# A two-layer diffusion backbone on one core: the recurrence's triangles loaded ahead of all rows, its rows a step ahead of its scores, the modulation read out by ScalarE, and the second layer's gated projections first

## The chip, the cores and the metric

The kernel runs on one core of a Trainium2 chip. The metric is the device time of one execution in microseconds (us); the program before has a median of 2315.48 us over three runs, from 2312.57 to 2316.03 us. The engines have short names: PE is TensorE (matmuls), PEld its weight loads, DVE is VectorE, ACT is ScalarE, POOL is GpSimd and SP is SyncE, which here only issues transfers. Each engine works through its own list of instructions in a fixed order.

## The reference

Two layers work on 512 latent tokens and 256 context tokens of width 1024. Each layer modulates its normalised input by a vector computed from the conditioning, projects it once, and feeds three token mixers: a bidirectional recurrence (RWKV-7), latent attention and windowed attention. Each mixer's result is gated, projected, merged and added back. All in fp32. Cut to what the change touches:

```python
mod = jax.nn.silu(c) @ ada_w + ada_b          # 3072 values for the latent tokens, and again for the context
shift, scale, gate = jnp.split(mod[:, None, :], 3, axis=-1)
h = rms_norm(x, norm_g) * (1.0 + scale) + shift
za, ga, zb, gb, zc, gc, zg = jnp.split(h @ w_in, list(IN_CUTS), axis=-1)
ya, yac = rwkv7_branch(za, zac, ...)          # the recurrence
def step(S, inp):                             # per token, per head, both directions
    r_t, w_t, k_t, v_t, kk_t, a_t = inp
    sa = jnp.einsum('bhvk,bhk->bhv', S, kk_t)
    S = (S * w_t[:, :, None, :] - sa[..., None] * (kk_t * a_t)[:, :, None, :]
         + v_t[..., None] * k_t[:, :, None, :])
    return S, jnp.einsum('bhvk,bhk->bhv', S, r_t)
```

## The kernel before

**Projections.** Every weight tile is loaded (L165), rounded by ScalarE to a high part `wh` (L168) and subtracted by GpSimd to a low part `wl` (L169); a product of fp32 numbers is then three matmuls into the PSUM tile `g` (`hh` by `wh`, `hl` by `wh`, `hh` by `wl`). `proj` copies `g` out to a tile `st`: a plain copy by ScalarE (L789) for the inputs of the attentions, tanh by ScalarE (L791) and a multiply-add by VectorE (L793) for the gates `ga`, `gb`, `gc`. It then stores `st` (L795). One call of `pace(n)` emits n steps of these projections; a step of the second layer is three matmuls of 512 columns. They are the filler with which the recurrence is interleaved.

**The recurrence** (`rwkv`) works in 12 chunks of 64 tokens, four to a group. For a chunk `rwkv_scores` loads the rows `BK` and `AR` (L625 to L634) and `UV` (L635, L636), multiplies them on PE into `scps`, masks those on VectorE (L656, L658), then transposes `BK` on PE into `bkp` (L664). For a group `rwkv_inverse` loads its triangles `TT` in four transfers (L674, L675), transposes them on VectorE (L681), inverts them in 60 dependent VectorE instructions (L690, L692), transposes back (L695, L696), copies a part on ScalarE (L698), and finishes on PE (`zp`, `yp`). `rwkv_step` carries the state from chunk to chunk: `Rp`, `Up`, `Sp`, `Yp` on PE with copies between. `readout` normalises finished rows and stores them.

**The modulation** (`ada`) runs beside this. The first layer's first four parts are computed at the start with a pool of their own; the other 16 rounds (four of the first layer, twelve of the second) are spread among the filler of the first layer. A round is PE products into `modps`, a copy of them to `row` (L269), four short matmuls with the constant `sum4`, and an add of the bias into `mod` (L277 or L280); both the copy and the add are VectorE's. The two halves of one PSUM bank take turns.

**Order.** A scheduler orders each engine by priority bands; inside `in_line()` PE takes the matmuls in the order in which the code emits them. `FILL[l]` says how many filler steps come ahead of the recurrence and inside each of its parts:

```python
FILL = ((48, 48, 2, (2, 2, 2), (3, 3, 3), 2), (72, 56, 4, (2, 2, 2), (3, 3, 3), 2))
```

Its fourth entry holds for the first three chunks of a group, three parts in each; the fifth for the last chunk. SP issues nearly all loads and stores from one list, so a transfer that waits for a buffer holds up those behind it.

Of the kernel before, what the change touches and what calls it, by code (L numbers as in the profile page):

```python
# [32 lines left out]
FILL = ((48, 48, 2, (2, 2, 2), (3, 3, 3), 2), (72, 56, 4, (2, 2, 2), (3, 3, 3), 2))  # L33
# [27 lines left out]
def build(tc, A, out):  # L61
# [165 lines left out]
    def ada(l, pp, mod, parts, pool=None):  # L227
# [30 lines left out]
        for i_, (q, h) in enumerate((q, h) for q in parts for h in range(512 // n)):  # L258
            ps = bank(i_)

            for k0 in range(0, KT, 4):
                with band(SERVE):
                    ws = four(q, h, k0)
                    for i in range(4):
                        mm(ps[32 * i:32 * i + 32], sc2[:, k0 + i, :], ws[i], start=(k0 == 0), stop=(k0 + 4 == KT),
                           skip_group_check=True)
                yield
            row = spool.tile([P, T], F32, tag="st", name="row", bufs=2)
            V.tensor_copy(row[:, 0:n], ps)  # L269
            nf = n // P  # L270
            pt = ps[:, 0:2 * nf].rearrange("p (f c) -> p f c", c=2)
            for i in range(nf):
                mm(pt[:, i, :], row[:, i * P:(i + 1) * P], C["sum4"])
            if q < 4:
                m, b = (a.rearrange("p (s f) c -> p s f c", s=2)[:, h:h + nf // 2, 2 * q:2 * q + 2]
                        for a in (mod[:, 0:16], pp[:, o:o + 16].unsqueeze(2)))
                V.tensor_tensor(m, pt.rearrange("p (s f) c -> p s f c", s=nf // 2), b.to_broadcast([P, nf // 2, 2, 2]), ALU.add)  # L277
            else:
                f = 4 * q + 2 * h
                V.tensor_tensor(mod[:, f:f + nf], pt, pp[:, o + f:o + f + nf].unsqueeze(2).to_broadcast([P, nf, 2]), ALU.add)  # L280
# [240 lines left out]
    def rwkv(l, D, last, DL, B, pace, zlast):  # L521

        with tc.tile_pool(name="rw", bufs=1, reuse_waits="tile") as rp:
            yo = rp.tile([P, 4, T], F32, name="yo")
            st = {"seen": set(), "S": None}
            parts, YB = {}, {}

            def scores(i):
                if i < NCH:
                    parts[i] = yield from rwkv_scores(l, last, rp, i)  # L530
# [11 lines left out]
            with band(B + 1):  # L542
                rest(scores(0), scores(1))
                ahead = invert(0)
                for _ in range(4):
                    next(ahead)
            with band(B + 4), tc.issue_after(zlast):
                pace(FILL[l][1])
            with band(B + 1), in_line():
# [3 lines left out]
                for i in range(NCH):  # L553
                    if i % NS == 0:
# [4 lines left out]
                        with band(B + 2):  # L559
                            for _ in range(3):  # L560
                                next(ahead, None)
                    nxt = scores(i + 2)
                    step = rwkv_step(l, last, i, yo, st, DL, rp, parts.pop(i), YB[i // NS])
                    for n in FILL[l][3 if i % NS < NS - 1 else 4]:
# [13 lines left out]
    def readout(l, D, rp, yo, part):  # L578
# [10 lines left out]
        tmp = rp.tile([P, 6, 256], F32, tag="AR", name="ro", bufs=4)  # L589
        def spread(p):  # L590
            ps = psum_bcast(256)
            mm(ps, bones, tmp[:, 4 + p % 2])
            V.tensor_scalar(tmp[:, p], ps, 1.0 / 64, None, ALU.mult)

        for p in range(4):
# [4 lines left out]
            S.activation(like(tmp[:, 4 + p % 2], y), y, AF.Square)  # L600
# [18 lines left out]
    def rwkv_scores(l, last, rp, i):  # L619
# [4 lines left out]
        UV = rp.tile([P, 2, 8, 64], F32, tag="UV", name="UV", bufs=4)  # L624
# [7 lines left out]
        else:  # L632
            for par, rows in enumerate(halves):
                DMA.dma_start(AR[rows, :, 2 * par], ar_d[l][rows, i, :, 0])  # L634
        DMA.dma_start(UV[OD, 0], v_d[l][:, i, 0])  # L635
# [844 lines left out]
    for l in range(2):  # L1480
# [18 lines left out]
        def tiles():  # L1499
# [5 lines left out]
            todo = (zb[2:] + zc[4:] + zc[:4] + zb[:2] if last else zb + zc) + ga + gb  # L1505
# [26 lines left out]
        if last:  # L1532
            cctx.close()
            with band(B + 3):
                gqa_tokens(l, F, last, ss)
        rwkv(l, D, last, DL, B, pace, zlast)
        weights["queue"] = getattr(nc, QUEUES[l][2])
        with band(B + 4), tc.issue_after(line["last"]):
            pace(22 * 8 - sum(FILL[l][0:2]) - 2 * FILL[l][2] - NG * (3 * sum(FILL[l][3]) + sum(FILL[l][4])) - 4 * FILL[l][5])
# [163 lines left out]
```

## Time and profile before

| | |
|---|---|
| median of 3 runs | 2315.48 us (2312.57 to 2316.03) |
| the profiled execution's own time | 2317.05 us |
| its span, first to last instruction | 2315.3 us |
| mean granted TensorE clock | 0.953 of full speed |
| PE busy | 2093.6 us, 90% of the span |
| PEld, DVE, ACT, POOL busy | 71%, 54%, 40%, 34% |
| matmuls in the profile | 16648 |
| first load of triangles, first layer | issued 341.66 us into the span |
| first load of triangles, second layer | issued 1583.35 us into the span |

The busy shares are means over stages of very different kinds. The granted clock is the share of full speed that the chip allowed TensorE. Idle time of an engine counts only where that engine holds up the end; in what follows that engine is PE, whose list is nearly full.

### The profile page before, as it was taken

How to read it: one execution, taken by the hardware profiler on the slowest of the kernel's cores; microseconds unless marked ns; L12 is line 12 of the kernel's file. 1: busy time of each engine (PE TensorE's matmuls, PEld its weight loads, DVE VectorE, ACT ScalarE, POOL GpSimd, SP SyncE). 2: the span in 40 equal slices, each digit the busy share in tenths (PEclk: the TensorE clock that was granted, in tenths of full speed). 3: DMA queues.
4: the chain of work that ended last, by engine and by line, in shares of the span. 5: the costliest groups of instructions: out<-in, count | busy, mean ns of one | idle time of the engine just before them, and what ended most of it. 6: DMA issues, size and time to landing. Idle time of an engine off the chain costs nothing. (4 is left out here: it accounts for less than half of the span.)

```text
span 2315.3 us, 42230 instructions
## 1 busy us (share of the span) xinstructions
PE 2093.6 (90%) x16648; PEld 1641.4 (71%) x16648; DVE 1258.3 (54%) x2342; ACT 919.2 (40%) x1694; POOL 787.4 (34%) x646
## 2 busy tenths in 40 slices
PE   6988899888998899999999998799878998998989
PEld 2866667676887777777777876677667876666767
DVE  4457415558435777314776255643667457674742
ACT  3355321233345443443433245542323455444422
POOL 0223112111122444444543323334211145455663
PEclk9999899899999999999999999999989999999999
DMA  7146666555333111455134414567554262115264
GB/s 249 60 134 178 200 197 188 133 147 135 90 105 103 69 46 51 147 165 166 57 102 135 144 51 125 157 209 189 147 117 113 87 214 90 64 50 178 82 196 141
DMA packets 321222, 301.61 MB, mean 130 GB/s; under 512 B 111744, under 2 KB 234368, under 8 KB 321024
## 3 DMA queue, kind: packets, MB, share of 16 engines
q1 hardware_dynamic: 303216, 269.29, 39.0%
q10 hardware_dynamic: 17808, 29.63, 4.0%
q8 instruction: 131, 2.15, 0.4%
q14 instruction: 67, 0.55, 0.1%
HBM read 207.34 MB, written 91.49 MB: 129 GB/s over the span
## 5 line engine op out<-in xcount | busy, mean ns | idle before, releaser
L169 POOL TENSOR_TENSOR wl<-wf,wh 128x512 fp32r<-128x512 f32 x316 | 439.4, 1392 | 1145.3 <-ACT wh L168 1059.4
L157 PE MATMUL g<-hh,wh 128*128 128x512 f32 (+1 forms) x1264 | 468.2, 370 | 11.3 <-DVE st L793 6.3
L157 PE MATMUL g<-hh,wl 128*128 128x512 f32 (+1 forms) x1264 | 454.9, 360 | 9.0 <-POOL wl L169 9.0
L157 PE MATMUL g<-hl,wh 128*128 128x512 f32 (+1 forms) x1264 | 453.0, 358 | 0.0
L168 ACT CAST wh<-wf 128x512 fp32r<-128x512 f32 x316 | 195.0, 619 | 419.5 <-PE g L157 183.6
L157 PEld LDWEIGHTS g<-hh,wh 128*128 128x128 f32 x1264 | 249.2, 197 | 59.1 <-issue 10.2
L157 PEld LDWEIGHTS g<-hh,wl 128*128 128x128 f32 x1264 | 248.6, 197 | 46.1 <-POOL wl L169 10.2
L157 PEld LDWEIGHTS g<-hl,wh 128*128 128x128 f32 x1264 | 249.3, 197 | 34.9 <-issue 4.7
L924 ACT ACTIVATE pe<-stp 128x256 f32<-128x256 f32 (+2 forms) x224 | 114.2, 521 | 171.2 <-PE stp L157 162.5
L928 POOL TENSOR_TENSOR acc<-acc,pe 128x512 f32<-128x512 f32 (+2 forms) x128 | 143.6, 1122 | 105.8 <-ACT pe L924 89.4
L895 DVE TENSOR_REDUCE mx<-mps 128x1 f32<-128x384 f32 (+2 forms) x256 | 123.7, 532 | 26.5 <-PE mps L157 25.7
L157 PE MATMUL yps<-pe,vh 128*64 128x256 f32 (+1 forms) x704 | 96.1, 379 | 0.0
L157 PE MATMUL g<-yh,wh 128*128 128x512 f32 (+1 forms) x224 | 82.8, 373 | 14.1 <-ACT yh L1387 8.6
L949 DVE RECIPROCAL rec<-sps 128x256 f32<-128x256 f32 (+1 forms) x48 | 71.4, 1489 | 43.6 <-PE sps L157 43.0
L656 DVE TENSOR_TENSOR AR<-scps,cst 64x256 f32<-64x256 f32 x96 | 40.1, 418 | 90.1 <-PE scps L157 89.0
L157 PE MATMUL gc<-hh,wh 128*128 128x512 f32 x192 | 79.2, 412 | 8.9 <-ACT hh L333 4.6
L157 PE MATMUL g<-yl,wh 128*128 128x512 f32 (+1 forms) x224 | 82.9, 372 | 3.0 <-POOL yl L1388 3.0
L157 PE MATMUL g<-yh,wl 128*128 128x512 f32 (+1 forms) x224 | 80.8, 365 | 0.0
L157 PE MATMUL scps<-AR,BK 64*128 64x128 f32 (+1 forms) x768 | 64.0, 293 | 16.7 <-DMA AR<-ard 14.2
L157 PE MATMUL gc<-hl,wh 128*128 128x512 f32 x192 | 78.4, 408 | 0.0
L791 ACT ACTIVATE st<-g 128x256 f32<-128x256 f32 (+1 forms) x108 | 56.5, 523 | 52.6 <-PE g L157 52.1
L157 PE MATMUL gc<-hh,wl 128*128 128x512 f32 x192 | 76.6, 399 | 0.0
(392 smaller groups left out, 4299.8 us busy)
## 6 DMA issues: line engine op xcount, KB each, us to landing
wf<-w_in SPq DMA_DIRECT2D x163, 256.0 KB, 2.9
wf<-ada_w SPq DMA_DIRECT2D x84, 256.0 KB, 4.1
wf<-w_in ACTq DMA_DIRECT2D x77, 256.0 KB, 3.0
bkd<-bk SPq DMA_DIRECT2D x16, 768.0 KB, 5.6
zt<-thzg SPq DMA_DIRECT2D x48, 256.0 KB, 3.3
wf<-w_bo SPq DMA_DIRECT2D x40, 256.0 KB, 3.1
thzg<-st SPq DMA_DIRECT2D x24, 384.0 KB, 2.4
vd<-t SPq DMA_DIRECT2D x64, 96.0 KB, 2.4
```

Of the source, the lines that this page charges most:

```text
L157: queued(TE.matmul(o, l, r, start=start, stop=stop, **kw))
L168: S.copy(wh, w32)
L169: eng.tensor_tensor(wl, w32, wh.bitcast(F32), ALU.subtract)
L656: V.tensor_tensor(AR[oth, pds, 2 * par, :], ps[oth, :, a0:a0 + 64], msk("ms", oth), ALU.mult)
L791: S.activation(t[:, sl], p, AF.Tanh, scale=0.5)
L895: V.tensor_reduce(mx, ps, AX.X, ALU.max)
L924: S.activation(e, st, AF.Exp, scale=scale)
L928: G.tensor_tensor(acc, keep.pop(0, acc), e, ALU.add)
L949: V.reciprocal(rec, sps)
```

## The change

It has five parts. (1) In the 16 later rounds of `ada` the copy to `row` and the add of the bias move from VectorE to ScalarE: one copy, and two activations of two columns each in place of one add of four. (2) The loads of the rows become a function of their own, `rwkv_rows`. The triangles of group 0 are loaded ahead of all rows, and each later chunk's rows are issued one step ahead of its scores. (3) The scratch tile of `readout` shrinks from 6 to 4 blocks and takes its buffer from the tag `BK` (3 buffers) where it took one from `AR` (4 buffers). (4) In the second layer the gate tiles `ga` come after the first four tiles of the filler and ahead of the other ungated ones, and `gqa_tokens`, which prepares the windowed attention, is emitted behind the first `pace` of the recurrence and no longer ahead of it. (5) In the second layer group 0 gets three filler steps in each part and no longer two: nine more steps, taken from those behind the recurrence.

```diff
-FILL = ((48, 48, 2, (2, 2, 2), (3, 3, 3), 2), (72, 56, 4, (2, 2, 2), (3, 3, 3), 2))
+FILL = ((48, 48, 2, ((2, 2, 2),) * 3, (3, 3, 3), 2), (72, 56, 4, ((3, 3, 3), (2, 2, 2), (2, 2, 2)), (3, 3, 3), 2))
...
-            V.tensor_copy(row[:, 0:n], ps)
+            (V.tensor_copy if pool else S.copy)(row[:, 0:n], ps)
...
-            if q < 4:
+            if pool:
...
-                f = 4 * q + 2 * h
-                V.tensor_tensor(mod[:, f:f + nf], pt, pp[:, o + f:o + f + nf].unsqueeze(2).to_broadcast([P, nf, 2]), ALU.add)
+                f = 8 * h + 2 * q if q < 4 else 4 * q + 2 * h
+                for i in range(nf):
+                    S.activation(mod[:, f + i, :], pt[:, i, :], AF.Identity, bias=pp[:, o + f + i:o + f + i + 1])
...
+            def rows(i):
+                if i < NCH:
+                    rows_[i] = rwkv_rows(l, last, rp, i)
...
             with band(B + 1):
+
+                ahead = invert(0)
+                next(ahead)
+                for i in range(2):
+                    rows(i)
                 rest(scores(0), scores(1))
-                ahead = invert(0)
-                for _ in range(4):
+                for _ in range(3):
                     next(ahead)
+                rows(2)
             with band(B + 4), tc.issue_after(zlast):
                 pace(FILL[l][1])
+            beside()
...
+                    rows(i + 3)
                     nxt = scores(i + 2)
...
-                    for n in FILL[l][3 if i % NS < NS - 1 else 4]:
+                    for n in FILL[l][3][i // NS] if i % NS < NS - 1 else FILL[l][4]:
...
-        tmp = rp.tile([P, 6, 256], F32, tag="AR", name="ro", bufs=4)
+        tmp = rp.tile([P, 4, 256], F32, tag="BK", name="ro", bufs=3)
...
-    def rwkv_scores(l, last, rp, i):
+    def rwkv_rows(l, last, rp, i):
...
+        return AR, BK
+
+    def rwkv_scores(l, last, rp, i, AR, BK):
...
-            todo = (zb[2:] + zc[4:] + zc[:4] + zb[:2] if last else zb + zc) + ga + gb
+            todo = zb[2:] + zc[4:] + ga + zc[:4] + zb[:2] + gb if last else zb + zc + ga + gb
...
-            with band(B + 3):
-                gqa_tokens(l, F, last, ss)
-        rwkv(l, D, last, DL, B, pace, zlast)
+
+        def tokens():
+            if last:
+                behind = line["last"]
+                with band(B + 3):
+                    gqa_tokens(l, F, last, ss)
+                line["last"] = behind
+
+        rwkv(l, D, last, DL, B, pace, zlast, tokens)
```

The scheduler turns this into a new order on several engines. Three places follow; line numbers of the changed kernel are some 1 to 19 higher than before (L693 and L694 are the loads L674 and L675, L700 is L681, L709 and L711 are L690 and L692, L714 and L715 are L695 and L696, L717 is L698, L675 and L677 are the masks L656 and L658, L812 and L814 are L793 and L795).

**First place: the first layer, ahead of the recurrence.** SP's list before, around the third and fourth load of the first group's triangles (`TT`); `wf` are weight tiles:

```order
L165 DMA wf<-w_in 128x512 [waits DMAHW6_49,DMAHW1_49,PE_49]
L254 DMA wf<-ada_w 128x2x256 [waits DMAHW2_49,Pool_49]
L674 DMA TT<-ttd_130 32x8x256
L254 DMA wf<-ada_w 128x2x256 [waits DMAHW4_49,PE_49]
L165 DMA wf<-w_in 128x512 [waits DMAHW5_49,PE_49]
L254 DMA wf<-ada_w 128x2x256 [waits DMAHW6_49,DMAHW3_49,Pool_49]
L675 DMA TT<-ttd_130 32x32x32
L795 DMA zbd_121<-st 128x768 [waits Activation_49]
```

and now, where the last load (L694) has moved 37 entries up its list, to just ahead of the store that was issued at 328.70 us before:

```order
L693 DMA TT<-ttd_130 32x8x256
L814 DMA zbd_121<-st 128x768 [waits Activation_49]
L254 DMA wf<-ada_w 128x2x256 [waits DMAHW5_49,Pool_49]
L165 DMA wf<-w_in 128x512 [waits DMAHW3_49,DMAHW2_49,PE_49]
L254 DMA wf<-ada_w 128x2x256 [waits DMAHW4_49,PE_49]
L254 DMA wf<-ada_w 128x2x256 [waits DMAHW6_49,PE_49]
L165 DMA wf<-w_in 128x512 [waits DMAHW1_49,PE_49]
L694 DMA TT<-ttd_130 32x32x32
L814 DMA zbd_121<-st 128x768 [waits DMAHW7_49,Activation_49]
```

VectorE's list now, at the end of that first inverse; before, the masks L656 and L658 of the first two chunks all stood ahead of the inverse:

```order
L709 TENSOR_TENSOR inv<-inv,YB 128x30 [waits DVE_49]
L711 TENSOR_TENSOR YB<-YB,inv 128x30 [waits DVE_49]
L714 STREAM_TRANSPOSE YB<-YB 128x32x32 [waits DVE_49]
L715 STREAM_TRANSPOSE inv<-YB 128x1024 [waits DVE_49]
L675 TENSOR_TENSOR AR<-scps,cst 64x4x64 [waits PE_49]
L677 TENSOR_TENSOR TR<-scps,cst 128x4x64
L675 TENSOR_TENSOR AR<-scps,cst 64x4x64 [waits PE_49]
L677 TENSOR_TENSOR TR<-scps,cst 128x4x64
```

All but the first two masks of these chunks have moved behind the inverse.

**Second place: the first layer, second inverse, at about 468 to 477 us of the profile before.** VectorE's list before, with the add L280 of a modulation round behind the inverse's first transpose back:

```order
L695 STREAM_TRANSPOSE YB<-YB 128x32x32 [waits DVE_49]
L656 TENSOR_TENSOR AR<-scps,cst 64x4x64 [waits DMAHW1_49,PE_49]
L658 TENSOR_TENSOR TR<-scps,cst 128x4x64
L656 TENSOR_TENSOR AR<-scps,cst 64x4x64 [waits PE_49]
L658 TENSOR_TENSOR TR<-scps,cst 128x4x64
L280 TENSOR_TENSOR mod_162<-modps,pp 128x4 [waits PE_49]
L696 STREAM_TRANSPOSE inv<-YB 128x1024 [waits DVE_49]
```

and ScalarE's list now at the same place, with the same round's two activations L281:

```order
L684 COPY BKs<-bkp 128x512 [waits PE_49] x2
L754 COPY Rs<-Rp 128x512 [waits PE_49,Activation_49]
L717 COPY YB<-YB 32x32x32 [waits DVE_49,Pool_49]
L281 ACTIVATE mod_162<-modps,pp 128x2 [waits PE_49]
L281 ACTIVATE mod_162<-modps,pp 128x2
L717 COPY YB<-YB 32x32x32
L760 COPY UV<-Up 64x512 [waits PE_49,Activation_49]
```

The add has moved to ScalarE, where it stands behind the copy L717, which waits for the same transpose.

**Third place: the second layer, ahead of its first inverse.** VectorE's list before:

```order
L431 TENSOR_TENSOR ks<-pr,vT 128x512 [waits PE_49]
L656 TENSOR_TENSOR AR<-scps,cst 64x4x64 [waits PE_49] x8
L793 SCALAR_TENSOR_TENSOR st<-st,g 128x512 [waits DMAHW4_49,DMAHW6_49,DMAHW1_49,Activation_49]
L681 STREAM_TRANSPOSE inv<-TT 128x1024 [waits DMAHW5_49,DMAHW7_49,DMAHW4_49,DMAHW2_49]
L686 MEMSET YB 128x32 [waits Pool_49]
```

and now:

```order
L432 TENSOR_TENSOR ks<-pr,vT 128x512 [waits PE_49]
L812 SCALAR_TENSOR_TENSOR st<-st,g 128x512 [waits DMAHW6_49,DMAHW4_49,Activation_49]
L812 SCALAR_TENSOR_TENSOR st<-st,g 128x512 [waits DMAHW6_49,Activation_49]
L812 SCALAR_TENSOR_TENSOR st<-st,g 128x512 [waits DMAHW5_49,Activation_49]
L812 SCALAR_TENSOR_TENSOR st<-st,g 128x512 [waits DMAHW4_49,Activation_49]
L700 STREAM_TRANSPOSE inv<-TT 128x1024 [waits DMAHW5_49,DMAHW7_49,DMAHW2_49,DMAHW1_49]
L705 MEMSET YB 128x32 [waits Pool_49]
```

The four gate tiles stand ahead of the inverse, and no longer one ahead of it and the others within; the eight masks stand within it now.

## Rows read from the trace of the kernel before

**Rows 1.** The page: PE's and the other engines' busy time, share, instructions.

```profile
PE 2093.6 (90%) x16648; PEld 1641.4 (71%) x16648; DVE 1258.3 (54%) x2342; ACT 919.2 (40%) x1694; POOL 787.4 (34%) x646
```

**Rows 2.** Windows: length, busy of PE, PEld, DVE, ACT, POOL; granted clock; DMA.

```profile
266.00:480.00 214.00, 183.76 (x1761) 140.27 (x1760) 88.30 (x216) 44.67 (x81) 38.41 (x32) 0.92 0.62 174
412.50:422.30 9.80, 9.55 (x155) 7.99 (x156) 1.60 (x5) 2.73 (x5) 0.59 (x1) 0.52 0.32 95
1275.00:1300.00 25.00, 25.00 (x146) 21.77 (x145) 6.63 (x10) 6.30 (x9) 7.80 (x7) 1.00 0.47 158
```

**Rows 3.** PE's waits, 262 to 582 us: total, times, longest.

```profile
PE scps L157 <- DMA AR<-ard: 14.2, 3, 7.3
PE modps L157 <- DMA wf<-ada_w: 7.5, 4, 5.8
PE modps L157 <- DVE mod L280: 6.6, 3, 6.1
...
PE zp L157 <- DVE inv L696: 2.4, 1, 2.4
...
PE g L157 <- DVE st L793: 1.7, 1, 1.7
```

**Rows 4.** PE's waits, 1600 to 1720 us.

```profile
PE zp L157 <- DVE inv L696: 10.8, 1, 10.8
PE zp L157 <- issue: 6.1, 1, 6.1
PE g L157 <- DVE st L793: 4.3, 2, 3.1
```

**Rows 5.** Timeline of VectorE at 263 us: start, duration, instruction, idle before.

```profile
263.87 0.15 DVE L280 TENSOR_TENSOR mod<-modps,pp 128x4 f32<-128x4 f32 x1
```

**Rows 6.** Timeline of VectorE, the first layer's first inverse.

```profile
372.82 1.98 DVE L681 STREAM_TRANSPOSE inv<-TT 128x1024 f32<-128x1024 f32 x1
...
406.19 1.93 DVE L695 STREAM_TRANSPOSE YB<-YB 128x1024 f32<-128x1024 f32 x1
408.15 1.25 DVE L696 STREAM_TRANSPOSE inv<-YB 128x1024 f32<-128x1024 f32 x1
```

**Rows 7.** Timeline of SP: a store of the filler, and the fourth triangle load.

```profile
328.70 0.34 SPq L795 DMA_DIRECT2D zbd<-st  x1
...
365.45 0.56 SPq L675 DMA_DIRECT2D TT<-ttd  x1
```

**Rows 8.** Timeline of PE ahead of the second chunk's scores.

```profile
354.35 0.39 PE L157 MATMUL g<-hl,wh 128*128 128x512 f32 x1
354.58 0.39 PE L157 MATMUL g<-hh,wl 128*128 128x512 f32 x1
354.81 0.50 PE L157 MATMUL modps<-cst,row 128*128 128x2 f32 x4
```

**Rows 9.** Timeline of three engines at the first layer's second inverse.

```profile
470.77 0.25 PE L157 MATMUL modps<-cst,row 128*128 128x2 f32 x1
...
475.51 2.11 ACT L698 COPY YB<-YB 32x1024 f32<-32x1024 f32 x2 [6.36 <-DVE YB L695]
...
476.89 0.14 DVE L280 TENSOR_TENSOR mod<-modps,pp 128x4 f32<-128x4 f32 x1
...
477.09 1.08 PE L157 MATMUL modps<-wf,sc 128*32 128x256 f32 x8 [6.07 <-DVE mod L280]
```

**Rows 10.** Timeline of SP, 542 to 565 us.

```profile
542.26 0.37 SPq L165 DMA_DIRECT2D wf<-w_in  x1
...
564.96 0.58 SPq L631 DMA_DIRECT2D AR<-ard  x1
```

**Rows 11.** Timeline of VectorE in the second layer, around its first inverse.

```profile
1601.80 0.69 DVE L793 SCALAR_TENSOR_TENSOR st<-st,g 128x512 f32<-128x512 f32 x1 [12.40 <-ACT st L791]
...
1641.28 1.22 DVE L696 STREAM_TRANSPOSE inv<-YB 128x1024 f32<-128x1024 f32 x1
```

**Rows 12.** Groups by line on ScalarE: the shortest activation in the trace.

```profile
L121 ACT ACTIVATE sc<-c 128x16 f32<-128x16 f32 x1 | 0.2, 217 | 0.0
```

More of the change, by code (lines that the diff above doesn't have):

```diff
@@ L519, in zphase, with rwkv @@
                 inside()
-    def rwkv(l, D, last, DL, B, pace, zlast):
+    def rwkv(l, D, last, DL, B, pace, zlast, beside):
         with tc.tile_pool(name="rw", bufs=1, reuse_waits="tile") as rp:
@@ L525, in rwkv @@
             st = {"seen": set(), "S": None}
-            parts, YB = {}, {}
+            parts, YB, rows_ = {}, {}, {}
+            def rows(i):
+                if i < NCH:
+                    rows_[i] = rwkv_rows(l, last, rp, i)
             def scores(i):
                 if i < NCH:
-                    parts[i] = yield from rwkv_scores(l, last, rp, i)
+                    parts[i] = yield from rwkv_scores(l, last, rp, i, *rows_.pop(i))
             def invert(g):
@@ L587, in like @@
             return a.rearrange("p (b t) -> p b t", b=y.shape[1])
-        tmp = rp.tile([P, 6, 256], F32, tag="AR", name="ro", bufs=4)
+        tmp = rp.tile([P, 4, 256], F32, tag="BK", name="ro", bufs=3)
         def spread(p):
             ps = psum_bcast(256)
-            mm(ps, bones, tmp[:, 4 + p % 2])
+            mm(ps, bones, tmp[:, p])
             V.tensor_scalar(tmp[:, p], ps, 1.0 / 64, None, ALU.mult)
@@ L599, in readout @@
             S.copy(y, like(ps, y))
-            S.activation(like(tmp[:, 4 + p % 2], y), y, AF.Square)
+            S.activation(like(tmp[:, p], y), y, AF.Square)
             if p:
@@ L623, in rwkv_scores @@
         BK = rp.tile([P, 8, 2, 64], F32, tag="BK", name="BK", bufs=3)
-        UV = rp.tile([P, 2, 8, 64], F32, tag="UV", name="UV", bufs=4)
         DMA.dma_start(BK[EV], bk_d[l][EV, i])
@@ L634, in rwkv_scores @@
                 DMA.dma_start(AR[rows, :, 2 * par], ar_d[l][rows, i, :, 0])
+        return AR, BK
+    def rwkv_scores(l, last, rp, i, AR, BK):
+        has_r = i >= 4 or not last
+        UV = rp.tile([P, 2, 8, 64], F32, tag="UV", name="UV", bufs=4)
         DMA.dma_start(UV[OD, 0], v_d[l][:, i, 0])
@@ L1533, in build @@
             cctx.close()
-            with band(B + 3):
-                gqa_tokens(l, F, last, ss)
-        rwkv(l, D, last, DL, B, pace, zlast)
+        def tokens():
[5 more added lines that the diff above has]
+        rwkv(l, D, last, DL, B, pace, zlast, tokens)
         weights["queue"] = getattr(nc, QUEUES[l][2])
         with band(B + 4), tc.issue_after(line["last"]):
-            pace(22 * 8 - sum(FILL[l][0:2]) - 2 * FILL[l][2] - NG * (3 * sum(FILL[l][3]) + sum(FILL[l][4])) - 4 * FILL[l][5])
+            pace(22 * 8 - sum(FILL[l][0:2]) - 2 * FILL[l][2] - 3 * sum(chain(*FILL[l][3])) - NG * sum(FILL[l][4]) - 4 * FILL[l][5])
         def gates():
```

## The prediction

> **What bounds the kernel now.** I read the page first: PE is busy 2093.6 us of the span [rows 1], so the end is set by PE's list and its holes. A window of dense filler shows PE without a hole, 146 matmuls in 25.00 us at full clock [rows 2]: there nothing is to be gained. Then I read PE's waits in the two recurrences, where the change acts. In the first (262 to 582 us) PE waits 14.2 us in three pieces for the rows `AR`, once 5.8 us for a weight tile of the modulation, once 6.1 us for the add L280, 2.4 us for the first inverse and 1.7 us for the multiply-add L793 [rows 3]. In the second (1600 to 1720 us) it waits 6.1 us ahead of the first inverse's `zp` (put down to "issue", but VectorE's L696 ends just before), 4.3 us in two pieces for L793, and 10.8 us for the second inverse [rows 4]. The timelines then say who is late. Last the granted clock: it is 0.52 in the 9.8 us behind the holes at the first inverse [rows 2], near the lower of its two levels (1.2 and 2.4 GHz), while PE is busy all the time, so a hole costs more than its own length.
>
> The sum is made against the profiled execution's own 2317.05 us, 1.6 us above the median of 2315.48.
>
> **Modulation on ScalarE.** Sixteen rounds lose a copy and an add on VectorE. A full add takes 0.15 us there [rows 5]; two ScalarE activations of two columns are bounded from below by nothing and taken as 0.22 us each from the nearest row, 128 by 16 [rows 12]. ScalarE is busy 44.67 of 214 us in this stretch [rows 2], so the 32 of them, 7 us in all, lie beside other work; if that cover were gone they would cost those 7 us. What matters is where the waits go.
>
> At 263.87 us the add stands in VectorE's list behind the preparation of the recurrence [rows 5]; on ScalarE it can run as soon as its matmuls are done, and the next round's products stand 19 matmuls further up PE's list, so their weight load, the 5.8 us wait, is issued earlier by about 19 x 0.23 = 4 us (0.23 us from one filler matmul to the next [rows 8]). The transfers around it are busy, so I take back 3 us, between 0 and 5.8.
>
> At 471 us I expect nothing. VectorE does the add at 476.89 us, behind the inverse, while PE was done with `sum4` at 470.77 plus 0.25 [rows 9]. In the new order the activations stand on ScalarE behind the copy L717 (L698 before), and that copy waits for the same inverse: it started at 475.51 us after 6.36 us of idleness [rows 9]. Two copies take 2.11 us, so after the first, at 476.6 us, the activations follow and end at about 477: the 6.1 us stay. The Trainium skill (TensorE: Matmul & The Clock Gate, the table ahead of its first section) calls ScalarE's and VectorE's queues strict first-in-first-out; the 6.36 us of ScalarE and the late add on VectorE agree with it. The Trainium skill (ScalarE: Activation LUTs, Rules for kernel authors) speaks against this part, since it wants adds on VectorE and budgets about 0.3 us for an activation; by that the 32 would be an estimated 10 us of ScalarE, still under cover, and this case's nearest row says 0.22.
>
> **Triangles ahead, first layer.** The inverse began at 372.82 us and ended with L696 at 408.15 plus 1.25 [rows 6]. Its fourth load was issued at 365.45 us; the new list has it ahead of the store issued at 328.70 [rows 7], so about 37 us earlier. The first two waits before the recurrence, 1.7 and 2.4 us [rows 3], go with it: **-4.0 us**. What is late next are the scores. Their masks now stand behind the inverse on VectorE. By the old clock minus 7 us (3 from the hole at 266 us, 4 for a chunk's scores that PE has not done yet at that point), the last load goes out at about 321 and lands some 3 us on, at 324. The inverse took 33.4 us from L681 to L695 [rows 6], about 3 of them in modulation and gate work that leaves; 324 + 30 + 3.2 gives 357 for its end. PE does the modulation round at 354.81 in the old clock [rows 8], 344 in the new (7 and another chunk's scores, 4), and has some 7 us of filler and scores from there to the transposes of `BK`, which need a mask done: 351. So a new wait of **+6 us**, between 0 (the inverse is quicker by the slow steps it shares with others) and 11 (it keeps its full length and the rows land late).
>
> **Rows a step ahead.** The hole of 7.3 us at 561 us [rows 3] is a load of `AR` issued behind readout's transfers, its last part at 564.96 us [rows 10]. The new list has those three transfers ahead of readout's, right behind the weight load issued at 542.26 [rows 10]. They land long before 561: **-7.3 us**; the bound below is a return of half, if the next chunk's rows, now behind those transfers, come late. The other two pieces of the 14.2, 6.9 us at 441 to 448, stay: there the new list has the same loads behind the same weight loads. The change of tag is costed at nothing, since no chunk's `BK` is needed within 20 us of its issue; if one were, it is the same 7 us.
>
> **Second layer.** Before, VectorE sat 12.40 us until the first gate tile's tanh and only then began the inverse, which ended at 1641.28 plus 1.22 [rows 11]; gate tiles stood within it, and PE waited for two of them. Now the four gate tiles come ahead of it, beside filler, the triangles are loaded ahead of the rows, and the inverse can start some 20 us sooner (three tiles of the filler less and the scores' work behind it). PE has the same 276 filler matmuls to do before `zp`. So 6.1 + 4.3 us go: **-10.4 us**, between -4.3 (the inverse stretches by waiting for its eight masks) and -10.4.
>
> Nine steps more in group 0 are 27 matmuls of 512 columns, 27 x 0.23 = 6.2 us [rows 8], placed where PE waits 10.8 us for the second inverse [rows 4] and taken from filler that has no holes. That inverse also no longer waits for a gate tile behind the first state (1.2 us before it). I take **-6.0 us**, between -3 and -7.
>
> **Clock.** After a hole the clock is at half for 3 to 10 us while PE is busy; that loses half of the time. For the holes that go I count 9.8 us (first inverse [rows 2]) and, from windows of the same kind behind each of the others, 3.6 (561), 3.0 and 4.7 (second layer), and half of 6.9 (266): 24.5 us, so **-12 us**, between 0 (other holes bring it back) and -16. The new hole brings one back: **+2.5**.
>
> Sum: -3.0 - 4.0 + 6.0 - 7.3 - 10.4 - 6.0 - 12.0 + 2.5 = -34.2, so 2317.05 - 34.2 = **2283 us**.
>
> **Rivals.**
> 1. *The holes only move.* The inverse is a chain of 60 dependent steps, and shortening the way to it lets PE meet another part of it: the masks cost 11 us, the second layer's inverse stretches (-4.3), and the clock gives back nothing. -3 - 4 + 11 - 7.3 - 4.3 - 3 = -10.6: **2306 us**. For it speaks that the 6.1 us at 471 stay for just this reason; against it that the new starts are 20 us and more earlier.
> 2. *The change does more than I grant:* the rows at 441 us come earlier after all and the add at 471 too. -34.2 - 6.9 - 6.1 and 5 of clock: **2265 us**. Against it stand the lists.
> 3. *Slower: the masks behind the first inverse.* If the fourth triangle load is held in SP's list until about where it was (365 us in the old clock, 358 in the new), the inverse ends at 358 + 3 + 33.2 = 394, and PE stands at `BK`'s transposes from 351: 43 us lost in place of 6. The other terms then give -42.7 in sum, with clock; with a longer half clock behind such a hole (+5) the time is **2322 us**. It decides at an issue about 5 us before the old place. For it: SP's list is held by weight tiles that wait for PE and GpSimd; against: the store next to the load went out at 328.70 [rows 7].
> 4. *A strictly ordered ScalarE costs more than VectorE did:* by the rule named above every copy behind an activation that waits for PE waits with it. Sixteen rounds with two waits of the size of `sum4` (0.6 us) are at most 19 us, were none covered; a third of it on PE's path gives **2289 us**, within the forecast's own range.
>
> **Chances and range.** The forecast with rival 4: 0.58 (own range 2270 to 2298). Rival 1: 0.18. Rival 2: 0.13. Rival 3: 0.11. A tenth on either side is left out by 2262 to 2310. A change of 0.2%, 4.6 us, is about what a measurement of this kernel can tell from none; below 2310.8 lie the first three cases but for a corner of rival 1: faster 0.82, same 0.07, slower 0.11.
>
> **What would show it.** Right: no wait for L696 or L793 ahead of the first `zp` in either layer; no wait for `AR` in the step of 561 us; the waits at 441 and at the second inverse of the first layer as before, the latter now named ScalarE L281; a wait of PE at `bkp` or `scps` with VectorE's L675 as its cause, 4 to 8 us, in the first layer; the second layer's `zp` of group 1 waiting about 4 us. Wrong: if the triangles are issued later than 335 us; if the half clock takes as many us as before; if the wait at the second inverse is gone, or the one at `bkp` is over 15 us.

## The result, and the profile after

The changed kernel takes **2282.36 us** (median of 4 runs, 2269.15 to 2285.37) against 2315.76 us for the kernel before on the same chip (4 runs): a ratio of 0.9855, 95% interval 0.9827 to 0.9883, or 33.4 us less. A repetition on another chip, `after_again` below, gave 0.9851. The forecast was 2283. The profiled run took 2285.37 us, its span is 2283.4 us.

The page of the changed kernel, busy time of the engines, and the line on its core's span and clock:

```profile
PE 2090.7 (92%) x16648; PEld 1640.3 (72%) x16648; DVE 1258.0 (55%) x2310; ACT 931.6 (41%) x1742; POOL 789.7 (35%) x646
core 0: 2283.4 us, clock 0.958
```

PE is busy 2.9 us less than in [rows 1] and the span is 31.9 us shorter: about 29 us of PE's idle time are gone. PE's waits in the first recurrence of the changed kernel, to be held against [rows 3] (total, times, longest, in us):

```profile
PE modps L157 <- ACT mod L281: 7.3, 5, 4.9
PE scps L157 <- DMA AR<-ard: 6.6, 3, 3.5
PE pr L157 <- DVE TR L677: 2.9, 1, 2.9
...
PE Rp L157 <- ACT UV L746: 2.3, 1, 2.3
```

The wait of 5.8 us for `ada_w` and those for the first inverse and the gate tile are gone. Of the three waits for `AR` the one of 7.3 us is gone; the two ahead of it, 6.9 us before, are still there with 6.4. The add that PE waited 6.1 us for is now ScalarE's L281, with 4.9. A narrower window, 330 to 400 us, has the new wait that I had priced at 6 us:

```profile
PE bkp L160 <- DVE TR L677: 0.7, 1, 0.7
```

PE's waits in the second recurrence, 1600 to 1720 us, to be held against [rows 4]:

```profile
PE gqm L160 <- ACT x L1235: 4.2, 1, 4.2
PE Rp L157 <- ACT UV L746: 3.5, 2, 2.2
PE zp L157 <- DVE inv L715: 2.8, 1, 2.8
```

Of the 6.1 and 4.3 us at the first inverse nothing is left. The 10.8 us at the second have become 4.2 and 2.8: PE now meets, just ahead of `zp`, the preparation of the windowed attention (`gqm`), whose copy L1235 waits for an instruction of VectorE (L1198) that stands behind steps of the inverse.

The timeline of the first layer's first inverse (start, duration), to be held against [rows 6] and [rows 7]: SP's last triangle load, VectorE's inverse, PE's transposes of `BK`.

```profile
317.20 0.56 SPq L694 DMA_DIRECT2D TT<-ttd  x1
...
320.46 2.04 DVE L700 STREAM_TRANSPOSE inv<-TT 128x1024 f32<-128x1024 f32 x1 [38.96 <-DMA TT<-ttd]
347.06 0.43 DVE L675 TENSOR_TENSOR AR<-scps,cst 64x256 f32<-64x256 f32 x1
...
351.03 1.98 DVE L714 STREAM_TRANSPOSE YB<-YB 128x1024 f32<-128x1024 f32 x1
353.04 1.25 DVE L715 STREAM_TRANSPOSE inv<-YB 128x1024 f32<-128x1024 f32 x1
...
352.31 2.05 PE L157 MATMUL scps<-AR,BK 64*128 64x128 f32 x24
355.06 0.68 PE L160 MATMUL bkp<-cst,BK 64*128 64x64 f32 x8 [0.70 <-DVE TR L677]
```

The inverse begins 52 us earlier than in [rows 6] and ends at 354.3 us; PE has finished the scores at 354.4 us. The two meet almost exactly. The second layer, VectorE:

```profile
1568.38 0.69 DVE L812 SCALAR_TENSOR_TENSOR st<-st,g 128x512 f32<-128x512 f32 x1 [4.26 <-ACT st L810]
1568.99 2.04 DVE L700 STREAM_TRANSPOSE inv<-TT 128x1024 f32<-128x1024 f32 x1
...
1609.19 1.25 DVE L715 STREAM_TRANSPOSE inv<-YB 128x1024 f32<-128x1024 f32 x1
1624.31 0.69 DVE L812 SCALAR_TENSOR_TENSOR st<-st,g 128x512 f32<-128x512 f32 x1 [13.88 <-ACT st L810]
```

That inverse ends at 1610.4 us where [rows 11] have 1642.5. Four gate tiles' multiply-adds (L812) stand ahead of it, the last at 1568.38 us, the next comes at 1624.31, and none stands within; PE waits for none of them in the list above. The first `zp` starts at 1628.12 us, so the inverse is ready 17.7 us before it is wanted.

### The profile page after: what moved, and what is told of

Its sections match the earlier page's. It is cut to its first block, busy times and chain, and to the rows that moved or that the text cites. A ratio compares the mean times of both kernels' runs of the same rounds, so it can differ in the third digit from the quotient of the medians.

```text
span 2283.4 us, 42263 instructions
## 1 busy us (share of the span) xinstructions
PE 2090.7 (92%) x16648; PEld 1640.3 (72%) x16648; DVE 1258.0 (55%) x2310; ACT 931.6 (41%) x1742; POOL 789.7 (35%) x646
## 5 line engine op out<-in xcount | busy, mean ns | idle before, releaser
L169 POOL TENSOR_TENSOR wl<-wf,wh 128x512 fp32r<-128x512 f32 x316 | 440.4, 1395 | 1135.6 <-ACT wh L168 1066.2
L157 PEld LDWEIGHTS g<-hh,wl 128*128 128x128 f32 x1264 | 250.0, 198 | 48.5 <-POOL wl L169 11.2
L709 DVE TENSOR_TENSOR inv<-inv,YB 128x30 f32<-128x30 f32 (+9 forms) x180 | 71.2, 396 | 10.1 <-issue 4.9
L947 POOL TENSOR_TENSOR acc<-pe 128x512 f32<-128x512 f32 (+1 forms) x48 | 53.5, 1116 | 65.7 <-ACT pe L943 60.9
```

The costliest lines, as they stand in the source:

```text
L157: queued(TE.matmul(o, l, r, start=start, stop=stop, **kw))
L169: eng.tensor_tensor(wl, w32, wh.bitcast(F32), ALU.subtract)
L709: V.tensor_tensor(t3, M3[:, j:j + 1, 0:j].to_broadcast([P, n, j]), YK[:, j + 1:32, j:j + 1].to_broadcast([P, n, j]), ALU.mult)
L947: G.tensor_tensor(acc, keep.pop(0, acc), e, ALU.add)
```

## The experiments

The theory going in was the prediction's own list: every part pays where its hole was. The rivals were that one part carries another's gain, or that a hole only moves. First four parts were undone one by one in the changed kernel (on one chip; the kernel before has 2319.65 us there); then, on another chip (before: 2313.18 us), the changed kernel again with three variants; at last parts put into the kernel before, singly and together, and one step beyond the changed kernel (before: 2317.89 us). Ratios are to the kernel before on the same chip.

**ada_on_vector.** The modulation back on VectorE.

```diff
-            (V.tensor_copy if pool else S.copy)(row[:, 0:n], ps)
+            V.tensor_copy(row[:, 0:n], ps)
...
-                for i in range(nf):
-                    S.activation(mod[:, f + i, :], pt[:, i, :], AF.Identity, bias=pp[:, o + f + i:o + f + i + 1])
...
+                V.tensor_tensor(mod[:, f:f + nf], pt, pp[:, o + f:o + f + nf].unsqueeze(2).to_broadcast([P, nf, 2]), ALU.add)
```

> The changed kernel with its first part undone: the 16 later modulation rounds are copied and added by VectorE again. Theory (this part is worth the one hole at 266 us and nothing at the second inverse): PE's wait for the modulation's weight tile comes back with 4 to 6 us, the wait at the second inverse of the first layer stays within 2 us of its 4.9 us or shrinks, and the time is 2283 + 4 to 9 = 2287 to 2292 us. Rival (VectorE, freed of 32 instructions, is what made the first inverses quick): PE waits for the first inverse's end or for masks behind it by 5 us or more, and the time is 2295 us or above.

2283.24 us, ratio 0.984 (0.9817 to 0.9863): nothing that can be measured is lost. PE's waits in this kernel's first recurrence:

```profile
PE modps L157 <- DMA wf<-ada_w: 6.1, 2, 5.8
PE modps L157 <- DVE mod L280: 4.0, 3, 3.5
PE pr L157 <- DVE TR L676: 3.5, 2, 2.9
PE modps L157 <- DVE mod L277: 3.5, 4, 1.6
PE scps L157 <- DMA AR<-ard: 2.9, 1, 2.9
```

The 5.8 us at 266 us are back, so it is this part that had removed them. But PE, 6 us later, then waits for `AR` once for 2.9 us and no longer twice for 6.4, and 3.5 in place of 4.9 at the second inverse. The hole was worth its length only until the next late load.

**triangles_late.** The first group's triangles behind the rows and the scores again.

```diff
-                ahead = invert(0)
-                next(ahead)
                 for i in range(2):
                     rows(i)
                 rest(scores(0), scores(1))
-                for _ in range(3):
+                ahead = invert(0)
+                for _ in range(4):
                     next(ahead)
```

> The changed kernel with the first group's triangles loaded behind the scores of the first two chunks again; rows still a step ahead, all else as changed. Theory (the early triangles end the holes ahead of both first inverses): waits for L696's successor ahead of the first zp come back, 2 to 5 us in the first layer and 3 to 7 us in the second, with half clock behind them; 2283 + 8 to 14 = 2291 to 2297 us. Rival (the moved gate tiles and the free VectorE did it, the loads' place does not matter): no wait ahead of either zp, 2281 to 2286 us.

2294.82 us, ratio 0.9905 (0.9872 to 0.9938), by the ratios some 11 us above the changed kernel, inside what the theory gave. Its waits, first in the first recurrence, then in the second:

```profile
PE zp L157 <- DVE inv L714: 6.6, 2, 4.6
...
PE g L157 <- DVE st L811: 2.4, 3, 1.4
```
```profile
PE g L157 <- DVE st L811: 7.2, 1, 7.2
```

In the second layer VectorE's first transpose starts at 1591.42 us (1568.99 in the changed kernel), and a gate tile's multiply-add stands behind nearly all of the inverse's steps, at 1623.71 us, though its tanh was done at 1612.7: PE waits 7.2 us for it. It is the fifth; the four that come first in the filler were done by 1570. So the wait is in the place where the theory had one ahead of `zp`, under another name. In the first layer `zp` waits 4.6 us and L811 1.4, but two holes of the changed kernel nearly go: the rows `AR` (6.4 us in two) cost one wait of 1.8, and L281 at the second inverse (4.9) 0.5. So how the 11 us divide between the layers isn't shown.

**order_back.** The second layer's filler order and the place of `gqa_tokens` as before.

```diff
-            todo = zb[2:] + zc[4:] + ga + zc[:4] + zb[:2] + gb if last else zb + zc + ga + gb
+            todo = zb[2:] + zc[4:] + zc[:4] + zb[:2] + ga + gb if last else zb + zc + ga + gb
...
-        rwkv(l, D, last, DL, B, pace, zlast, tokens)
+            with band(B + 3):
+                gqa_tokens(l, F, last, ss)
+        rwkv(l, D, last, DL, B, pace, zlast, lambda: None)
```

> The changed kernel with the second layer's filler order and the place of gqa_tokens as before; triangles and rows ahead, nine steps more in group 0. Theory (in the second layer the gate tiles' place is worth the waits for the multiply-add, 4.3 us, the early triangles the 6.1 us ahead of zp): the waits of PE for the multiply-add come back with 2 to 5 us, none ahead of zp; 2283 + 3 to 8 = 2286 to 2291 us. Rival (the gate tiles held the inverse, so their place is worth the 6.1 us too): a wait of 4 us or more ahead of zp as well and 2293 us or above.

2281.3 us, ratio 0.9831 (0.9811 to 0.9852): theory and rival are both wrong. Neither the gate tile's wait nor the one ahead of the first `zp` returns; the window 1600 to 1720 us begins with

```profile
PE gqm L160 <- ACT x L1235: 4.2, 1, 4.2
PE zp L157 <- DVE inv L715: 2.8, 1, 2.8
PE Rp L157 <- DMA UV<-vd: 2.2, 1, 2.2
```

just as in the changed kernel. VectorE at the end of that inverse:

```profile
1601.22 0.69 DVE L812 SCALAR_TENSOR_TENSOR st<-st,g 128x512 f32<-128x512 f32 x1
...
1604.54 1.25 DVE L715 STREAM_TRANSPOSE inv<-YB 128x1024 f32<-128x1024 f32 x1
```

In the old order two gate tiles do stand within the inverse (1588.85 and 1601.22 us), but it begins at 1561.32 and is over at 1605.8, 16 us ahead of the first `zp` at 1621.85. With the triangles early there is room for them, and their order doesn't matter.

**fill_back.** Two steps in each part of the second layer's first group.

```diff
-FILL = ((48, 48, 2, ((2, 2, 2),) * 3, (3, 3, 3), 2), (72, 56, 4, ((3, 3, 3), (2, 2, 2), (2, 2, 2)), (3, 3, 3), 2))
+FILL = ((48, 48, 2, ((2, 2, 2),) * 3, (3, 3, 3), 2), (72, 56, 4, ((2, 2, 2),) * 3, (3, 3, 3), 2))
```

> The changed kernel with two filler steps in each part of the second layer's group 0 as before (27 matmuls go back behind the recurrence). Theory (they lie in the wait for the second inverse): that wait and the ones in group 0 grow by 5 to 6.5 us in sum, the time to 2283 + 4 to 8 = 2287 to 2291 us. Rival (the inverse starts later by as much as the filler takes, so nothing is hidden): 2281 to 2285 us.

2296.43 us, ratio 0.9902 (0.9874 to 0.9931), by the ratios about 11 us above the changed kernel, the wait back at its old size:

```profile
PE zp L157 <- DVE inv L715: 11.3, 1, 11.3
```

The sign and the place are as expected, the size is nearly twice the -6.0 of the sum, and little of it is found at that wait. From the first inverse's `zp` to the second's the kernel here takes 62.3 us and the changed kernel 64.6: the 27 matmuls, 6.2 us of work, lengthen that stretch by 2.4 us. The gain is found elsewhere. The 27 matmuls (25 of them in the records) came from the stretch of the attentions, from latent attention's first `mps` to the gates' first `gc`. That stretch in the kernel before, here, and in the changed kernel (length, busy of PE, PEld, DVE, ACT, POOL, clock, DMA):

```profile
1980.90:2231.20 250.30, 239.12 (x1352) 171.17 (x1351) 163.02 (x264) 106.21 (x208) 145.06 (x123) 0.99 0.32 100
```
```profile
1954.10:2205.20 251.10, 238.18 (x1351) 171.16 (x1349) 163.20 (x264) 106.17 (x208) 145.14 (x123) 0.99 0.32 101
```
```profile
1963.10:2200.80 237.70, 230.75 (x1327) 166.40 (x1326) 165.96 (x264) 103.83 (x205) 142.88 (x121) 0.99 0.33 102
```

The stretch is 12.6 to 13.4 us shorter with 25 (24) matmuls less, where 25 x 0.23 us are 5.8. PE's busy time falls by 8.4 us and its idle time there, 11.2 us before, by 4.2: a wait of 4.1 us for ScalarE's L1387 (5.2 us here, as L1406) is no longer among its waits. Why PE's busy time falls by more than the matmuls' 5.8 us was not followed. It is no accident of one profile: in the profiles of all four kernels with two steps (before, this one, `triangles_only`, `scratch_only`) the stretch is 250 to 253 us; in those of eight kernels with three steps, the changed kernel and its repetition among them, it is 237 to 239, and 242.5 in `inverse_copy_on_gpsimd`. Some 13 us gained there and 2.4 lost in the recurrence make the 11.

**after_again, rows_on_time, inverse_copy_on_gpsimd, only_loads_and_steps** ran together. The first is the changed kernel unchanged. In the second each chunk's rows are loaded by its own scores, as before; the smaller scratch tile stays:

```diff
 def scores(i):
+    rows(i)
     parts[i] = yield from rwkv_scores(l, last, rp, i, *rows_.pop(i))
...
-                    rows(i + 3)
```

In the third GpSimd copies the part of the inverse that stood on ScalarE ahead of L281:

```diff
-            S.copy(YB[b0:b0 + 32, :, 32:64], YB[b0:b0 + 32, :, 0:32])
+            G.tensor_copy(YB[b0:b0 + 32, :, 32:64], YB[b0:b0 + 32, :, 0:32])
```

The fourth has the edits of `ada_on_vector` and `order_back` together.

> The changed kernel unaltered, as the measure for the others of this group on the same chip. Both theories: a ratio to the kernel before of 0.983 to 0.988, and the same holes of PE: 6 to 7 us for the rows ahead of the second inverse, about 5 us at that inverse behind ScalarE, about 7 us in two pieces at the second layer's second inverse.

> The changed kernel with each chunk's rows loaded by its own scores again, not a step ahead; triangles still first, readout's scratch still in the rows' other tag. Theory (the step ahead ended the hole of 7.3 us at 561): a wait of PE for the rows of 5 to 8 us comes back there and the time is 4 to 8 us above the changed kernel run beside it. Rival (the new tag of the scratch tile frees the buffer early enough and the scheduler moves the loads up by itself): no wait over 2.5 us there and a time within 3 us of the changed kernel.

> The changed kernel with the inverse's two copies, behind which the modulation's activations stand on ScalarE, done by GpSimd. Theory (at the first layer's second inverse PE waits for activations that are held by those copies): the wait of 4.9 us for L281 falls below 1.5 us, and the time is 3 to 8 us below the changed kernel run beside it, if GpSimd's weight parts are not held up in turn. Rival (PE meets the inverse itself there, whichever engine reads): the wait moves to another name, stays at 4 us or more in sum, and the time is within 3 us of the changed kernel.

> The kernel before with the triangles first, the rows a step ahead, readout's scratch moved and nine steps more in group 0; the modulation stays on VectorE and the second layer's order as it was. Theory, after the runs that undid those two parts one by one: they add nothing, and the time is within 5 us of the changed kernel run beside it. Rival (each hides the lack of the other, since both free VectorE around the inverses): PE waits for the multiply-add or ahead of a zp by 5 us or more and the time is 8 us or more above.

| | median (range), us | ratio (95%) |
|---|---|---|
| after_again | 2279.78 (2277.81 to 2281.43) | 0.9851 (0.9832 to 0.987) |
| rows_on_time | 2280.8 (2276.25 to 2287.27) | 0.9858 (0.9831 to 0.9885) |
| inverse_copy_on_gpsimd | 2283.77 (2275.66 to 2287.49) | 0.9864 (0.9836 to 0.9891) |
| only_loads_and_steps | 2279.95 (2276.69 to 2286.47) | 0.9861 (0.9835 to 0.9888) |

`rows_on_time` loses nothing. Its waits in the step of the old 7.3 us hole, 540 to 582 us:

```profile
PE scps L157 <- DVE TR L674: 1.9, 1, 1.9
PE Rp L157 <- ACT UV L743: 1.0, 1, 1.0
```

No wait for `AR`: the rows a step ahead are not what removed it. `only_loads_and_steps` equals the changed kernel, so the modulation on ScalarE and the second layer's order add nothing that can be measured here, even together. In `inverse_copy_on_gpsimd` the waits for the modulation in the first recurrence fall from 7.3 to

```profile
PE modps L157 <- ACT mod L281: 3.0, 5, 1.2
```

which shows that the 4.9 us were L281's wait for the copy ahead of it on ScalarE; by the total there is still no gain.

**scratch_only.** The kernel before with the smaller scratch tile in `BK` and nothing else.

```diff
-        tmp = rp.tile([P, 6, 256], F32, tag="AR", name="ro", bufs=4)
+        tmp = rp.tile([P, 4, 256], F32, tag="BK", name="ro", bufs=3)
...
```

> The kernel before with one edit: readout's scratch tile takes 4 blocks from the tag BK and no longer 6 from AR. My prediction gave the 7.3 us hole at 561 us to the rows being issued a step ahead; the run with rows loaded by their own scores kept the gain, so the theory is now that the scratch tile did it, by not holding an AR buffer. Theory: with this edit alone PE's wait for AR at about 561 us falls from 7.3 to under 2.5 us, all other waits stay, and the time is 6 to 10 us below the kernel before (ratio 0.9955 to 0.9975). Rival: the tag is not enough by itself and the wait at 561 us stays above 5 us, same time.

2311.68 us (12 runs), ratio 0.9981 (0.9963 to 0.9998): by the ratio 4.4 us (0.5 to 8.6). SP in that step, to be held against [rows 10], and PE's waits there:

```profile
545.18 0.57 SPq L629 DMA_DIRECT2D AR<-ard  x1
545.81 1.32 SPq L631 DMA_DIRECT2D AR<-ard  x2
```
```profile
PE scps L157 <- DVE TR L658: 2.2, 1, 2.2
PE Rp L157 <- ACT UV L727: 1.4, 1, 1.4
```

The three loads of `AR` go out at 545 to 547 us, ahead of readout's transfers; in [rows 10] the last is at 564.96. In the kernel before SP stands 11.3 us ahead of the first of them (L629, issued at 555.45 us), until PE's `Yp`, which reads an older `AR`, is done, which I read as a wait for a buffer. The scratch tile no longer takes one of those buffers. The hole of 7.3 us is replaced by 2.2 and 1.4 us for the mask and the state copy that are late next, which leaves 3.7 us (7.3 - 2.2 - 1.4), well within what was measured and less than I had expected for it.

**triangles_only.** The kernel before with the triangles loaded ahead of all rows (rows, as in `rows_on_time`, by their own scores). One thing more differs: the scratch tile has 4 blocks here, not 6, though still in the tag `AR`.

```diff
+                ahead = invert(0)
+                next(ahead)
                 rest(scores(0), scores(1))
-                ahead = invert(0)
-                for _ in range(4):
+                for _ in range(3):
                     next(ahead)
...
-        tmp = rp.tile([P, 6, 256], F32, tag="AR", name="ro", bufs=4)
+        tmp = rp.tile([P, 4, 256], F32, tag="AR", name="ro", bufs=4)
```

> The kernel before with one edit: the triangles of the first group are issued ahead of all rows, in both layers; rows, scratch tile, modulation, filler counts and filler order as before. Theory (triangles carry what I gave to the second layer's order as well): no wait of PE for VectorE's transpose back or for the gate multiply-add ahead of the first zp, in the first layer (4.0 us before) and the second (10.4 us before); the waits of 7.3 us for AR at 561 us and 10.8 us at the second layer's second inverse stay; the time is 10 to 18 us below the kernel before (ratio 0.992 to 0.996). Rival (the new filler order is needed too, as I had argued for the second layer): the second layer's waits stay above 6 us and the gain is under 7 us.

2303.45 us, ratio 0.9942 (0.9921 to 0.9964): by the ratio 13.4 us, as the theory had it. In the second recurrence the gate tile and the first `zp` are gone from PE's waits, with the old filler order, and the second inverse is as it was:

```profile
PE zp L157 <- DVE inv L711: 10.8, 1, 10.8
PE Rp L157 <- ACT UV L742: 3.9, 2, 2.5
PE zp L157 <- DVE TR L673: 1.2, 1, 1.2
```

In the first recurrence PE's wait for `AR` in the step of the old hole stays, with 8.2 us. So the smaller scratch tile does not remove that hole as long as it is in `AR`; in `scratch_only` it was the tag.

**three_parts.** The kernel before with triangles first, the scratch tile, and the filler steps.

> The kernel before with three edits: triangles first, the scratch tile in BK with 4 blocks, and three filler steps for the second layer's first group. Rows on time, modulation on VectorE, filler order as before. Theory: these three carry the whole gain, so the time is that of the changed kernel, 31 to 37 us below the kernel before (ratio 0.984 to 0.9875). Rival (rows ahead, ScalarE and the new order matter together though not singly): at least 6 us short of that, ratio 0.9885 or more.

2289.62 us, ratio 0.9883 (0.9866 to 0.9901), by the ratio 27.1 us below before. That lies between the two expectations, nearer to the rival's bound; but `only_loads_and_steps`, which differs from it only in the rows a step ahead, had 0.9861 on another chip, and the intervals overlap. Whether some 5 to 7 us hang on the parts that show nothing singly stays open.

**gpsimd_and_four_steps.** The changed kernel with GpSimd's copy and nine steps more in the second layer's first group.

```diff
-FILL = ((48, 48, 2, ((2, 2, 2),) * 3, (3, 3, 3), 2), (72, 56, 4, ((3, 3, 3), (2, 2, 2), (2, 2, 2)), (3, 3, 3), 2))
+FILL = ((48, 48, 2, ((2, 2, 2),) * 3, (3, 3, 3), 2), (72, 56, 4, ((4, 4, 4), (2, 2, 2), (2, 2, 2)), (3, 3, 3), 2))
```

> The changed kernel with two edits: the copy of the inverse's part goes from ScalarE to GpSimd, and the second layer's first group gets four filler steps in each part in place of three. Theory: the remaining wait of PE at the second layer's second inverse (2.8 us zp and 4.2 us behind it in the changed kernel) shrinks by 3 us or more, the wait of 4 to 5 us at 458 us is gone, and the time is 5 to 12 us below the changed kernel (ratio 0.980 to 0.983). Rival: what is taken out there comes back as other waits or in the filler behind, and the ratio stays within 0.984 to 0.988.

2296.39 us, ratio 0.9914 (0.9893 to 0.9936): some 14 us slower than the changed kernel. The rival has the direction, and the loss is larger than it said. The wait at the second inverse did shrink, to 1.7 us. The loss is behind the recurrence. The stretch from the last `Yp` to the first `trp`, in which the latent attention is prepared, in the changed kernel and here:

```profile
1829.60:1933.60 104.00, 93.77 (x412) 73.10 (x406) 63.59 (x137) 66.04 (x122) 44.32 (x36) 0.97 0.48 155
```
```profile
1823.90:1945.90 122.00, 105.19 (x460) 83.13 (x456) 62.60 (x141) 68.49 (x130) 49.13 (x40) 0.96 0.47 152
```

It grew by 18.0 us. Among PE's waits, 1820 to 1990 us, is now one for GpSimd, which makes the low part `wul` of the latent attention's weights with the same L169 as the filler's:

```profile
PE qps L157 <- POOL wul L169: 6.2, 2, 5.2
PE pr L157 <- DVE yo L791: 4.7, 1, 4.7
```

PE did 48 matmuls more in this stretch; the stretch behind it, up to `gc`, took 265.5 us with 1351 matmuls against 267.2 with 1422: PE's idle time in it went from 13.6 to 23.9 us, so it gave next to nothing back for 71 matmuls less. That the attentions' own chain holds it is my reading and was not tried. GpSimd's copy alone did not move the preparation: in `inverse_copy_on_gpsimd` the same stretch takes 102.7 us with 412 matmuls, as many as in the changed kernel. So it needs the nine steps; whether they do it without GpSimd's copy was not run.

## Why the prediction was right, and where it was not

The total was right, and so was the list of holes that go; four of the reasons were not (rows, the second layer's order, FILL, modulation). Errors of size balanced: of the terms, -3.0 came out as nothing, -7.3 as about -4.4, +6 as about +1, -6.0 as about -11. That the total came within 1 us is luck in part.

- **Triangles ahead, first layer (-4.0).** Right for the waits (4.1 us in [rows 3]): both are gone, and return when only this is undone. What that is worth in the first layer by itself is not shown, since other waits there go when they return.
- **The new wait (+6).** Mis-sized: 0.7 us, and 1.3 us in `after_again`. The mechanism, masks behind the inverse, is what the trace shows; I had the inverse end at 357 us and PE arrive at 351. They were 354.3 and 354.4. The bound of 0 held.
- **Rival 3, the slower one,** needed the last load to be issued near 358 us; it was 317.20 us, against my 321. **Rival 4** (6 us more for ScalarE's order) does not show either: with the modulation on VectorE the time is the same. Its 0.6 us for `sum4` is 0.50 in [rows 8].
- **Rows a step ahead (-7.3).** The step failed in its cause. I gave the hole to the loads being emitted earlier and costed the change of tag at nothing. `rows_on_time` and `scratch_only` show the reverse: the tag alone is enough, and the rows a step ahead are not needed. Whether the rows a step ahead would have been enough without the tag was not run. The size was too large too: 3.7 us by the waits, 4.4 by the time.
- **Second layer (-10.4).** Those waits went, but I named three causes, and the triangles alone are enough: `order_back` keeps the gain and `triangles_only` has it. I read the 12.40 us ahead of the inverse in [rows 11] as a wait for the gate tile's tanh. But the last triangle load went out only at 1596.71 us there, and loads of `TT` took 3.5 to 5.9 us to land in that layer, so without the gate tile the inverse at 1602.40 could have begun little sooner. The order of the gates is not needed once the inverse ends 16 us ahead of `zp`, with or without gate tiles in it.
- **FILL (-6.0).** The hole shrank by 3.8 us only (10.8 to 2.8 and 4.2), since a wait for ScalarE's L1235 stands ahead of it, while 6.2 us of work were put there: the recurrence itself lost 2.4 us. Yet undoing this part costs about 11 us. The step that failed is "taken from filler that has no holes": that stretch had 11.2 us of idle time, and became 13 us shorter without the 27 matmuls, where I had counted 6.2. Nine steps more, with GpSimd's copy, lost 14 us. It is a question of which stretch gives, and how much it has.
- **Modulation (-3.0).** The hole at 266 us went, as worked out, and more of it than I took, but it was given back at the loads of `AR` and at the second inverse; net nothing. At the second inverse I had expected 6.1 us to stay behind L717, and 4.9 did. The timeline there:

```profile
457.85 0.50 PE L157 MATMUL modps<-cst,row 128*128 128x2 f32 x4
...
461.67 1.04 ACT L717 COPY YB<-YB 32x1024 f32<-32x1024 f32 x1 [5.20 <-DVE YB L714]
...
462.74 0.41 ACT L281 ACTIVATE mod<-modps,pp 128x2 f32<-128x2 f32 x2
...
463.21 1.08 PE L157 MATMUL modps<-wf,sc 128*32 128x256 f32 x8 [4.86 <-ACT mod L281]
```

  ScalarE is idle 5.20 us at L717, L281's operands have been ready since 458.35 us, when PE was done with `sum4`, and the wait goes when L717 goes to GpSimd. The Trainium skill (TensorE: Matmul & The Clock Gate, the table ahead of its first section) calls ScalarE's queue strictly first-in-first-out; these rows and that run agree.
- **The price of an activation.** 0.26 us each (253 to 263 ns, 32 of them), so 8.3 us of ScalarE in all, where my row's 0.22 gave 7. It lay under cover, as costed. The Trainium skill (ScalarE: Activation LUTs, Rules for kernel authors) budgets about 0.3 us for an activation; the measured 0.26 is close to it.
- **Clock (-12 and +2.5).** PE's busy time fell by 2.9 us in the first profile and by 11.5 (to 2082.1) in `after_again`. The term's 9.5 us lie between the two, and one profile of either kernel doesn't fix it. A lowered clock behind a hole is still there: with PE busy 9.26 of 9.30 us behind the second layer's second inverse, the granted clock is 0.68, between its two levels (1.2 and 2.4 GHz):

```profile
1692.70:1702.00 9.30, 9.26 (x185) 7.66 (x185) 2.09 (x4) 3.97 (x7) 3.17 (x3) 0.68 0.23 72
```

So the gain is made of three parts: triangles first (13.4 us alone, 11 when undone), the filler steps (11 when undone), the scratch tile (4.4 alone). They sum to 26 to 29 us of the 33; `three_parts` measures 27.1. The modulation on ScalarE, the rows a step ahead and the second layer's order singly show nothing that these runs can tell from none.

## What to carry to other kernels

When several edits land together, each hole that goes has several possible causes; ask of each edit alone whether it would be enough, pool tags and buffer counts included: a scratch tile that shares a tag with prefetched rows was the cause here, not the order of the loads. Remove a hole early in a stretch and look at what is late next, since a wait for a transfer further on takes it back. Filler moved into a hole is to be priced at both ends: here 6.2 us of work cost 2.4 us around the hole and saved 13 us in the stretch it came from, and nine steps more, with one other edit, cost about as much as the first nine had gained.

## What the runs showed of the hardware that was not expected

- The same program has a PE busy time of 2090.7 us in one profiled execution and 2082.1 in another on another chip, with a granted clock of 0.958 and 0.963 and spans of 2283.4 and 2277.8 us. A term of a few microseconds can't be read from one pair of profiles.
- In the inverse's chain on VectorE a step now and then takes over 1 us where its like take 0.4 at most. In the changed kernel 18 of the 360 steps (6 inverses of 60) do, and each of the 18 overlaps GpSimd's subtraction L169, which began before it; 18 more steps overlap a GpSimd instruction and are not slow, and of the 324 that overlap none no step is. One of them, with its neighbour of the same shape, and GpSimd at that time:

```profile
1678.72 0.38 DVE L709 TENSOR_TENSOR inv<-inv,YB 128x210 f32<-128x210 f32 x1
...
1679.61 1.48 DVE L711 TENSOR_TENSOR YB<-YB,inv 128x210 f32<-128x210 f32 x1
```
```profile
1679.59 1.27 POOL L169 TENSOR_TENSOR wl<-wf,wh 128x512 fp32r<-128x512 f32 x1 [7.35 <-ACT wh L168]
```

  That is about 1.1 us for each, 3 of them in an inverse. It was seen, and not tried by an experiment.
